# Cross-covariance attention on one core: the K side scaled on GpSimd, logits behind the Gram products, V one unit deeper, closing transposes in other banks

## The chip, the core and the metric

One Trainium2 chip, of which the kernel uses one core. The metric is the device time of one execution in microseconds (us); lower is better. Four executions of the kernel before took 133.0 to 134.84 us, with a median of 133.59 us.

## The reference

Inputs are Q, K and V, each 8 x 12 x 512 x 64 in float32 (batch, heads, sequence, dim). The attention is taken between channels, not between positions:

```python
Q_norm = Q / (np.linalg.norm(Q, axis=-2, keepdims=True) + 1e-10)
K_norm = K / (np.linalg.norm(K, axis=-2, keepdims=True) + 1e-10)
attn = np.einsum('bhnd,bhne->bhde', Q_norm, K_norm)
attn = np.exp(attn - np.max(attn, axis=-1, keepdims=True))
attn = attn / (np.sum(attn, axis=-1, keepdims=True) + 1e-10)
return np.einsum('bhnd,bhde->bhne', V, attn)
```

For each of the 96 heads this is a 64 x 64 matrix of products over 512 positions, a softmax over its rows, and a product of V with it.

## The kernel before

The 96 heads are taken four at a time, so there are 24 units. A unit loads 512 KB each of Q, K and V and stores 512 KB. All 97 transfers are issued by the one queue of SyncE (SP), in the order in which the program writes them.

For unit u the work is this. VectorE (DVE) casts Q and K to bf16 side by side into one tile `qkb` (`cast_q`, line 80, and `cast_k`, line 83). TensorE (PE) multiplies each head's [Q K] with itself, 64 small matmuls into the four-bank PSUM tile `gbuf`, named gram (`grams`, line 94). The diagonal holds the squared norms, the lower left block K^T Q. `norms` takes the diagonal of each head on VectorE (line 106, four instructions) and raises it to the power -1/2 on GpSimd (POOL) (line 111, tile `rq`). `keep_kq` copies the K^T Q block out of PSUM on ScalarE (ACT) (line 99). `scale_k` multiplies it by K's factors (line 116, on VectorE, tile `kqs`), `logits` transposes it on TensorE (line 122, tile `lgdup`), `scale_q` multiplies by Q's factors (line 126), `exps` is the exponential on ScalarE (line 130), and `normalise` sums, inverts and multiplies on VectorE (lines 134, 136, 138, tile `ab`). `doubled` brings a copy of the result to the other 64 partitions, by a matmul with the identity (line 152) and a copy on ScalarE (line 153).

V has its own path. `cast_v` makes it bf16 (line 87, on ScalarE in the loop, on VectorE for the last four units). `vtrans` transposes it with eight TensorE instructions into the PSUM tile `vps` (line 145) and copies it out on ScalarE (line 147, tile `vt`). `outs` multiplies `vt` by `ab` in two halves into two PSUM buffers `po` (line 163) and copies each half to `so` (line 167); `store` writes it.

The order on every engine is the order of the program; no scheduler moves anything. The main loop runs steps s = 0 to 23 (lines 199 to 226). In step s the calls are: loads of Q and K of unit s + 3; loads of V up to unit n1 + 2; stores up to n1 - 4; casts of the new V; `cast_q(s+1)`, `scale_k(s-1)`, `normalise(s-2)`, `grams(s)`, `norms(s)`, `cast_k(s+1)`, `doubled(s-2)`, `keep_kq(s)`, the `outs` that are due, `logits(s-1)`, `scale_q(s-1)`, `exps(s-1)` and the new `vtrans`. Here n1 = `outs_by(s)` counts the units whose `outs` are done by the end of step s; it is 19 after the last step. Lines 227 to 260 then close: `scale_k`, `logits`, `scale_q` and `exps` of unit 23, `normalise` and `doubled` of units 22 and 23, and `outs` of units 19 to 23. In this closing part, copies of `outs` are split between ScalarE and VectorE from unit 20 on.

Buffers matter here: Q and K have five each, V five (`vp`), `vb` four, `vt` three, the output ten. `vps` has one buffer of one bank, `gram` has four banks. `lgdup` is one bank: the logits lie in partitions 0 to 63 of its first half, the doubled matrix in partitions 64 to 127 of its second half.

Of the kernel before, what the change touches and what calls it, by code (L numbers as in the profile page):

```python
# [9 lines left out]
BF16 = mybir.dt.bfloat16  # L10
# [5 lines left out]
HU = 4  # L16
NV = 32
R = 16
SV = 2
MV = 64  # L20
TP = 4
# [3 lines left out]
def kernel(  # L25
# [7 lines left out]
    nc = tc.nc  # L33
    B, H, N, _ = Q.shape
    assert N == NV * R and Q.shape[3] == D
    U = B * H // HU
# [5 lines left out]

    const = ctx.enter_context(tc.tile_pool(name="const", bufs=1))
    qp = ctx.enter_context(tc.tile_pool(name="qp", bufs=5))
    vp = ctx.enter_context(tc.tile_pool(name="vp", bufs=5))
    vbp = ctx.enter_context(tc.tile_pool(name="vbp", bufs=4))
    qkp = ctx.enter_context(tc.tile_pool(name="qkp", bufs=4))
    vtp = ctx.enter_context(tc.tile_pool(name="vtp", bufs=3))
# [3 lines left out]
    ps_v = ctx.enter_context(tc.tile_pool(name="ps_v", bufs=1, space=bass.MemoryType.PSUM))  # L52
# [5 lines left out]
    def outs_by(s):  # L58

        return max(0, (s - 2) * 10 // 11)  # L60
# [10 lines left out]
    def load_v(u):  # L71
        vf[u] = vp.tile([128, SV, TP * 2 * D], F32, name="vf")
        nc.sync.dma_start(out=vf[u], in_=Vf[u])

    def store(u, g=slice(0, SV)):
        nc.sync.dma_start(out=Of[u][:, g], in_=so[u][:, g].rearrange("p s t d -> p s (t d)"))
# [8 lines left out]
    def cast_v(u, copy=nc.scalar.copy):  # L85
        w = vb[u] = vbp.tile([128, SV, TP, 2 * D], BF16, name="vb")
        copy(w.rearrange("p s t d -> p s (t d)"), vf[u])  # L87
# [25 lines left out]
    def scale_k(u):  # L113

        kk = kqs[u] = small.tile([128, HU, D], F32, name="kqs")
        nc.vector.tensor_tensor(  # L116
            out=kk[D:], in0=kq[u][D:], in1=rq[u][D:, :, None].to_broadcast([D, HU, D]), op=ALU.mult,
        )

    def logits(u):  # L120
        for h in range(HU):
            nc.tensor.transpose(lg[:, h, :], kqs[u][D:, h, :], ident[D:, D:])  # L122
# [14 lines left out]
        a = abuf[u % len(abuf)]  # L137
        nc.vector.tensor_tensor(out=a[0:D, :, 0, :], in0=ex[u], in1=ri[:, :, None].to_broadcast([D, HU, D]), op=ALU.mult)  # L138

    def vtrans(u):  # L140

        ps = ps_v.tile([128, SV, TP, 128], BF16, name="vps")
        for g in range(SV):
            for t in range(TP):
                nc.tensor.transpose(ps[:, g, t, :], vb[u][:, g, t, :], identb)  # L145
        w = vt[u] = vtp.tile([128, SV, TP, 128], BF16, name="vt")
        nc.scalar.copy(w, ps)  # L147

    def doubled(u):

        a = abuf[u % len(abuf)]
        nc.tensor.matmul(dup[D:], identb[0:D, 0:D], a[0:D, :, 0, :], tile_position=(0, D))  # L152
        nc.scalar.copy(a[D:, :, 1, :], dup[D:])  # L153

    def outs(u, copies=(nc.scalar.copy, nc.scalar.copy)):
        s = so[u] = sop.tile([128, SV, TP, 2 * D], F32, name="so")
        a = abuf[u % len(abuf)]
        for g in range(SV):
            po = ps_o.tile([128, TP, 2 * D], F32, name="po")
            for t in range(TP):  # L160
                for x in range(2):
                    rows = slice(MV * x, MV * (x + 1))
                    nc.tensor.matmul(  # L163
                        po[rows, t, :], vt[u][:, g, t, rows],
                        a[:, 2 * g + x].rearrange("p a d -> p (a d)"), tile_position=(0, MV * x),
                    )
            copies[g](s[:, g], po)  # L167

    gbuf = ps_g.tile([128, HU, 512], F32, name="gram")
# [20 lines left out]
    def on(f, u):  # L190
        if 0 <= u < U:
            f(u)
# [5 lines left out]
    nv, nst, nt = 2, 0, 0  # L198
    for s in range(U):
        n0, n1 = outs_by(s - 1), outs_by(s)  # L200
        on(load_qk, s + LOAD_AHEAD)
        while nv < min(U, n1 + 3):
            load_v(nv)
            nv += 1
        while nst < n1 - 3:
            store(nst)
            nst += 1
        new = range(nt, n1 + 1) if s >= 1 else ()
        for v in new:
            cast_v(v)  # L210
        on(cast_q, s + 1)
        on(scale_k, s - 1)
        on(normalise, s - 2)
        on(grams, s)
        on(norms, s)
        on(cast_k, s + 1)
        on(doubled, s - 2)
        on(keep_kq, s)
        for v in range(n0, n1):
            outs(v)  # L220
        on(logits, s - 1)
        on(scale_q, s - 1)
        on(exps, s - 1)
        for v in new:
            vtrans(v)
            nt = v + 1
# [8 lines left out]

    last = U - 1
    both = (nc.scalar.copy, nc.vector.tensor_copy)
    scale_k(last)
    logits(last)
    cast_v(n1 + 1, nc.vector.tensor_copy)  # L240
    normalise(last - 1)
# [1 line left out]
    exps(last)  # L243
    outs(n1)
    store(n1)
    vtrans(n1 + 1)
    doubled(last - 1)
    normalise(last)
    doubled(last)
    cast_v(n1 + 2, nc.vector.tensor_copy)  # L250
    for u in range(n1 + 1, U):
        if u + 1 < U:
            vtrans(u + 1)
        if u + 2 < U:
            cast_v(u + 2, nc.vector.tensor_copy)
        outs(u, both)
        if u < last:
            store(u)
# [32 lines left out]
```

## Time and profile before

| | before |
|---|---|
| time, median of four | 133.59 us |
| time of the profiled execution | 133.54 us |
| span in that profile | 131.7 us |
| busy: PE, DVE, ACT, POOL | 68%, 76%, 70%, 32% |
| HBM traffic | 50.3 MB, 382 GB/s over the span |
| mean granted TensorE clock | 0.846 |

The span runs from the first to the last instruction of the program; 1.84 us of the execution's time lie outside it. A row of groups gives the line, the engine, the operation, its tiles and shapes, how often it ran, its busy time and mean duration, and the idle time of the engine ahead of it with what ended that idle time. A row of the timeline gives start, duration, engine, line and operation, and in brackets the idle time before it and its releaser. The stage table gives, for stretches of the span, each engine's busy time (with the number of instructions), then the granted clock, the share of DMA engine time and GB/s.

### The profile page before, as it was taken

The page shows a single profiled execution, that of the slowest core. Times are in us where ns is not written, and L with a number is a line of the kernel's source. Part 1 is how long each engine was busy: PE and PEld are TensorE (multiplying, and loading weights), DVE is VectorE, ACT ScalarE, POOL GpSimd, SP SyncE. Part 2 cuts the span into 40 slices and gives each one's busy share as a digit, 9 for nine tenths or more (in the row PEclk, how much of TensorE's full clock was granted, in tenths as well). Part 3 has the DMA queues.
Part 4 walks back from the last instruction along what each step waited for, and adds up shares of the span by engine and source line. Part 5 has one row for each costly group of instructions (what it writes and reads, how often), then busy time and mean ns, then how long its engine had stood idle before and what let it go on. Part 6 is the DMA issues. An engine that isn't in the chain of part 4 may idle for free.

```text
span 131.7 us, 5371 instructions
## 1 busy us (share of the span) xinstructions
PE 89.8 (68%) x2232; PEld 70.0 (53%) x2232; DVE 100.7 (76%) x368; ACT 92.0 (70%) x161; POOL 41.9 (32%) x41
## 2 busy tenths in 40 slices
PE   0057855799669475959965499666889639577930
PEld 0046733577457354838743387455668528355730
DVE  0757789878899997948999979999979776682540
ACT  3002722478999999849896488999986969866560
POOL 7704432541444323405422363234440430300000
PEclk9999999999999999655899757999856995955595
DMA  4999999999999999999999999999999999998665
GB/s 153 379 417 402 399 409 410 404 397 399 402 397 411 405 417 404 407 400 410 404 415 405 413 409 409 411 407 410 403 415 404 407 405 402 407 403 320 236 262 218
DMA packets 20008, 50.67 MB, mean 385 GB/s; under 512 B 1552, under 2 KB 1552, under 8 KB 19984
## 3 DMA queue, kind: packets, MB, share of 16 engines
q1 hardware_dynamic: 19984, 50.34, 97.9%
q8 instruction: 17, 0.28, 0.8%
q14 instruction: 7, 0.06, 0.1%
HBM read 37.75 MB, written 12.58 MB: 382 GB/s over the span
## 4 chain that ended last, share of the span: by engine, by line
PE 26%; DMA 26%; DVE 24%; POOL 11%; issue 6%; ACT 4%; POOLq 0%; ACTq 0%; DVEq 0%; SPq 0%
DMA vf<-in_V_dram 23%; POOL rq L111 11%; PE gram L94 11%; DVE scr L106 7%; PE vps L145 6%; PE po L163 5%; DVE esum L134 3%; DVE ab L138 3%; DVE kqs L116 3%; DMA qf<-in_Q_dram 3%; PE lgdup L122 2%; ACT vt L147 2%; PE lgdup L152 2%; DVE qkb L80 2%; DVE qkb L83 1%
## 5 line engine op out<-in xcount | busy, mean ns | idle before, releaser
L111 POOL TENSOR_TENSOR rq<-nsq,mhalf 128x4 f32<-128x4 f32 x24 | 36.8, 1532 | 71.5 <-DVE nsq L106 71.5
L94 PE MATMUL gram<-qkb 32*128 32x128 bf16 x1536 | 36.7, 260 | 14.1 <-DVE qkb L83 9.1
L94 PEld LDWEIGHTS <-qkb 32*128 32x128 bf16 x1536 | 30.5, 116 | 18.6 <-DVE qkb L83 9.9
L106 DVE CUSTOM_DVE_ANT_0 scr<-gram,ident 128x128 f32<-128x128 f32 x96 | 22.0, 281 | 5.3 <-PE gram L94 5.1
L147 ACT COPY vt<-vps 128x1024 bf16<-128x1024 bf16 x24 | 24.0, 1002 | 2.4 <-PE vps L145 2.0
L167 ACT COPY so<-po 128x512 f32<-128x512 f32 x44 | 23.8, 588 | 0.8 <-PE po L163 0.4
L87 ACT CAST vb<-vf 128x1024 bf16<-128x1024 f32 x20 | 20.9, 1046 | 4.9 <-DMA vf<-in_V_dram 4.9
L80 DVE CAST qkb<-qf 128x1024 bf16<-128x1024 f32 x24 | 17.9, 745 | 5.6 <-DMA qf<-in_Q_dram 5.5
L163 PEld LDWEIGHTS <-vt 128*64 128x64 bf16 x384 | 14.9, 134 | 12.9 <-ACT vt L147 7.9
L145 PE MATMUL vps<-identb,vb 128*128 128x128 bf16 x192 | 19.4, 262 | 1.3 <-ACT vb L87 0.7
L163 PE MATMUL po<-ab,vt 128*64 128x128 bf16 x384 | 19.3, 259 | 1.1 <-DVE so L167 0.8
L152 PE MATMUL lgdup<-ab,identb 64*64 64x256 bf16 x24 | 8.0, 334 | 16.0 <-DVE ab L138 14.4
L145 PEld LDWEIGHTS <-vb 128*128 128x128 bf16 x192 | 14.6, 118 | 5.5 <-issue 1.6
L153 ACT CAST ab<-lgdup 64x256 bf16<-64x256 f32 x24 | 8.8, 367 | 11.4 <-PE lgdup L152 11.1
L99 ACT COPY kq<-gram 64x256 f32<-64x256 f32 x24 | 8.8, 367 | 11.1 <-DVE nsq L106 10.6
L83 DVE CAST qkb<-kf 128x1024 bf16<-128x1024 f32 x24 | 16.4, 683 | 0.0
L122 PE MATMUL lgdup<-ident,kqs 64*64 64x64 f32 x96 | 11.9, 256 | 5.0 <-ACT ab L153 3.4
L126 DVE TENSOR_TENSOR sl<-lgdup,rq 64x256 f32<-64x256 f32 x24 | 9.9, 414 | 5.7 <-PE lgdup L122 5.1
L130 ACT ACTIVATE ex<-sl 64x256 f32<-64x256 f32 x24 | 10.0, 417 | 4.4 <-DVE sl L126 4.2
L122 PEld LDWEIGHTS lgdup<-ident,kqs 64*64 64x64 f32 x96 | 7.3, 126 | 9.2 <-ACT ab L153 6.3
L116 DVE TENSOR_TENSOR kqs<-kq,rq 64x256 f32<-64x256 f32 x24 | 10.1, 422 | 2.6 <-ACT so L167 0.8
L134 DVE TENSOR_REDUCE esum<-ex 64x4 f32<-64x256 f32 x24 | 9.9, 411 | 1.2 <-ACT ex L130 0.5
(16 smaller groups left out, 36.5 us busy)
## 6 DMA issues: line engine op xcount, KB each, us to landing
qf<-in_Q_dram SPq DMA_DIRECT2D x24, 512.0 KB, 10.4
kf<-in_K_dram SPq DMA_DIRECT2D x24, 512.0 KB, 10.4
vf<-in_V_dram SPq DMA_DIRECT2D x24, 512.0 KB, 10.2
out_dram<-so SPq DMA_DIRECT2D x23, 512.0 KB, 10.1
out_dram<-so SPq DMA_DIRECT2D x2, 256.0 KB, 2.6
```

Source lines behind the costliest of these rows:

```text
L80: nc.vector.tensor_copy(qkb[u][:, :, 0:D], qf[u])
L83: nc.vector.tensor_copy(qkb[u][:, :, D:], kf[u])
L87: copy(w.rearrange("p s t d -> p s (t d)"), vf[u])
L94: nc.tensor.matmul(gbuf[:, h, 0:2 * D], x, x, start=(t == 0), stop=(t == R - 1), tile_position=(NV * h, 0))
L106: nc.vector.tensor_tensor_reduce(out=scr, in0=gbuf[:, h, 0:2 * D], in1=ident, scale=1.0, scalar=1e-20, op0=ALU.mult, op1=ALU.add, accum_ou ...
L111: nc.gpsimd.tensor_tensor(out=r, in0=n2, in1=mhalf, op=ALU.pow)
L116: nc.vector.tensor_tensor(out=kk[D:], in0=kq[u][D:], in1=rq[u][D:, :, None].to_broadcast([D, HU, D]), op=ALU.mult,)
L122: nc.tensor.transpose(lg[:, h, :], kqs[u][D:, h, :], ident[D:, D:])
L145: nc.tensor.transpose(ps[:, g, t, :], vb[u][:, g, t, :], identb)
L147: nc.scalar.copy(w, ps)
L163: nc.tensor.matmul(po[rows, t, :], vt[u][:, g, t, rows], a[:, 2 * g + x].rearrange("p a d -> p (a d)"), tile_position=(0, MV * x),)
L167: copies[g](s[:, g], po)
```

## The change

Four things change.

1. `scale_k` runs on GpSimd, and for unit s in step s, so it stands directly behind `norms(s)`'s power in GpSimd's order. Its call before the closing part goes.
2. In a step, `logits(s-1)`, `scale_q(s-1)` and `exps(s-1)` come directly after `keep_kq(s)`. So TensorE's order becomes grams, logits, outs, doubled, vtrans (before: grams, doubled, outs, logits, vtrans). ScalarE's order becomes keep_kq, exps, outs' copies, doubled's copy, vtrans' copy (before: doubled's copy, keep_kq, outs' copies, exps, vtrans' copy). On VectorE `cast_k(s+1)` comes behind `scale_q(s-1)` in place of ahead of it.
3. V is loaded up to unit n1 + 3, with six buffers in place of five.
4. In the closing part, `vtrans` of units 20 to 23 writes to the four banks of `gbuf` in turn (banks 0, 1, 2, 3) in place of `vps`.

```diff
-    vp = ctx.enter_context(tc.tile_pool(name="vp", bufs=5))
+    vp = ctx.enter_context(tc.tile_pool(name="vp", bufs=6))
...
-        nc.vector.tensor_tensor(
+        nc.gpsimd.tensor_tensor(
             out=kk[D:], in0=kq[u][D:], in1=rq[u][D:, :, None].to_broadcast([D, HU, D]), op=ALU.mult,
         )
...
-    def vtrans(u):
+    def vtrans(u, bank=None):
 
-        ps = ps_v.tile([128, SV, TP, 128], BF16, name="vps")
+        if bank is None:
+            ps = ps_v.tile([128, SV, TP, 128], BF16, name="vps")
+        else:
+            ps = gbuf[:, bank].bitcast(BF16).rearrange("p (s t c) -> p s t c", s=SV, t=TP)
...
-        while nv < min(U, n1 + 3):
+        while nv < min(U, n1 + 4):
             load_v(nv)
...
         on(cast_q, s + 1)
-        on(scale_k, s - 1)
         on(normalise, s - 2)
         on(grams, s)
         on(norms, s)
-        on(cast_k, s + 1)
-        on(doubled, s - 2)
         on(keep_kq, s)
-        for v in range(n0, n1):
-            outs(v)
+        on(scale_k, s)
         on(logits, s - 1)
         on(scale_q, s - 1)
         on(exps, s - 1)
+        on(cast_k, s + 1)
+        for v in range(n0, n1):
+            outs(v)
+        on(doubled, s - 2)
...
-    scale_k(last)
     logits(last)
...
-    vtrans(n1 + 1)
+    vtrans(n1 + 1, 0)
...
         if u + 1 < U:
-            vtrans(u + 1)
+            vtrans(u + 1, (u - n1) % HU)
```

## Prediction, made before the changed kernel ran

> **What bounds the kernel now.** I read the page's busy shares first, then its slices for DMA, because 50.3 MB is much for one core.
>
> ```profile
> PE 89.8 (68%) x2232; PEld 70.0 (53%) x2232; DVE 100.7 (76%) x368; ACT 92.0 (70%) x161; POOL 41.9 (32%) x41
> ...
> DMA  4999999999999999999999999999999999998665
> GB/s 153 379 417 402 399 409 410 404 397 399 402 397 411 405 417 404 407 400 410 404 415 405 413 409 409 411 407 410 403 415 404 407 405 402 407 403 320 236 262 218
> ```
>
> No engine is full, but the DMA engines are, at about 405 GB/s, until the last four slices. SP's timeline has issues 1.27 us apart (512 KB each) and its waits are on earlier transfers; a Q load issued at 94.03 is used at 104.21. So from 3 to 118 us the order and number of transfers set the pace, and work done faster in the middle buys nothing. Only the end can be shortened. The stage table of the end:
>
> ```profile
> 116.00:118.00 2.00, 1.80 (x19) 1.14 (x15) 1.45 (x5) 1.33 (x4) 0.00 (x0) 0.50 1.05 407
> 118.00:120.00 2.00, 0.62 (x5) 0.44 (x6) 1.39 (x3) 1.52 (x4) 0.00 (x0) 0.50 0.98 373
> 120.00:122.00 2.00, 1.84 (x25) 1.50 (x24) 0.24 (x1) 1.34 (x3) 0.00 (x0) 0.50 0.74 282
> 122.00:124.00 2.00, 1.88 (x24) 1.55 (x23) 1.12 (x3) 1.33 (x3) 0.00 (x0) 0.50 0.57 216
> 124.00:126.00 2.00, 1.72 (x24) 1.36 (x23) 0.81 (x2) 1.33 (x2) 0.00 (x0) 0.67 0.63 240
> ```
>
> The queue runs dry from 120 us: stores wait for `outs`. TensorE (first column) is busy 1.84 and 1.88 of 2 us, at half clock (0.50). The last copy ends at 127.92, its store is issued at about 128.1, and the span ends at 131.7: 3.8 us behind the last copy. So the time is decided by when the closing chain ends. Its links in the timeline:
>
> ```profile
> 106.77 1.04 ACT L87 CAST vb<-vf 128x1024 bf16<-128x1024 f32 x1 [1.04 <-DMA vf<-in_V_dram]
> 108.26 0.63 PE L122 MATMUL lgdup<-ident,kqs 64*64 64x64 f32 x4 [0.92 <-ACT ab L153]
> 113.14 1.01 POOL L111 TENSOR_TENSOR rq<-nsq,mhalf 128x4 f32<-128x4 f32 x1 [4.37 <-DVE nsq L106]
> 114.18 0.42 DVE L116 TENSOR_TENSOR kqs<-kq,rq 64x256 f32<-64x256 f32 x1 [0.83 <-ACT so L167]
> 116.67 0.42 ACT L130 ACTIVATE ex<-sl 64x256 f32<-64x256 f32 x1 [1.31 <-DVE sl L126]
> 120.81 1.01 ACT L147 COPY vt<-vps 128x1024 bf16<-128x1024 bf16 x1 [0.66 <-PE vps L145]
> 121.88 1.01 PE L145 MATMUL vps<-identb,vb 128*128 128x128 bf16 x8 [0.16 <-ACT vt L147]
> 124.05 1.01 PE L145 MATMUL vps<-identb,vb 128*128 128x128 bf16 x8 [0.16 <-ACT vt L147]
> 127.23 0.69 DVE L167 COPY so<-po 128x512 f32<-128x512 f32 x1 [0.73 <-PE po L163]
> ```
>
> V of unit 18 comes late (first row), which delays the doubled copy and so the logits (second). VectorE then waits for the power (third, fourth), ScalarE stands 1.31 us for the last exponential (fifth), and the last units alternate transposes and copies (the rest).
>
> [...] the first Q cast took 2.25 us in place of 0.69 while GpSimd's memsets ran, and the power takes 1.01 us alone but 1.46 (median), ending just behind a cast (65.75 behind a cast that ends at 65.72). But that cast began at 65.04, inside the power[...]. [...] logits wait for the copy of the doubled matrix (second row above), which lies in other partitions of that bank. [...] the grant changes at multiples of 3.4 us and was 0.50 from 115.1 to 125.3.
>
> **Scaling on GpSimd.** VectorE loses 24 x 0.42 = 10.1 us, 0.42 a step. The trace shows no such GpSimd instruction. [...] I take 0.7. In the middle: norms end at N, the power is through at N + 1.8 (behind two casts), the scaled tile at N + 2.5. The next logits follow the next grams, at N + 3 or later, so this is hidden under grams; without that cover it would cost TensorE 0.5 us a step. No DMA is issued by GpSimd, and only powers stand behind it.
>
> **The new order.** Logits no longer wait for a doubled copy of the same step (3.4 us of such waits on its matmuls in all). In return `doubled` waits for `scale_q`, with only vtrans behind it, and ScalarE's exponential waits for `scale_q`, about 0.1 us. ScalarE does some 4.0 us of work a step either way (0.37 + 1.07 + 0.42 + 1.0 + 1.05 + 0.37 less overlap). VectorE's step falls from 4.02 to about 3.6, TensorE's at half clock stays 4.9; transfers need 4 x 1.27 = 5.1 in the late part. So the middle stays with DMA: gain zero. If the cover failed, each step over 5.1 us would count in full.
>
> **V one deeper.** One V load moves ahead of Q and K of unit 4 on SP and everything behind it shifts by one transfer: Q of unit 23 lands at 104.2 + 1.3 = 105.5, V of unit 18 at 106.7 - 3.8 = 102.9, stores one place later. V of unit 23 keeps its place in the order, at 118.3. The sixth buffer is free in time (V of unit 17 is cast by 103). So the wait for V goes, and what is late next is Q: VectorE in step 22 runs Q's cast from 105.5, normalise and norms to 108.2 (0.7 + 1.0 + 1.0). Before, norms of that step ended at 107.4, but ScalarE's `keep_kq` began at 108.1 because of V. Now it begins at 108.25: no gain so far.
>
> **The closing part.** ScalarE is then busy without a gap. From start to start (as in the timeline of before), keep_kq, exponential, two outs copies, doubled copy, `vt` and `cast_v` take 0.39 + 0.43 + 0.96 + 0.35 + 0.91 + 1.05 = 4.1, and the same in step 23 up to `vt` 0.39 + 0.4 + 0.96 + 0.35 + 1.0 = 3.1, so `vt` of unit 19 ends at 115.45, as before (115.36). Norms of unit 23 end near 112.2, scaled tile at 114.0, logits behind the doubled copy at 114.5, `scale_q` to 115.5, exponential at 115.6 in place of 116.67. TensorE's outs of unit 19 (1.06) and transposes of 20 (1.03) end at 117.6; ScalarE's copy `vt` of 20 begins at 117.65, against 117.94: gain 0.3. Then units 20 to 23 go at TensorE's pace, 1.03 + 1.06 = 2.1 us a unit at half clock. Before it was 2.17 (121.88 to 124.05), with a wait of 0.16 on the one `vps` bank. With four banks the two waits go: gain up to 0.3, of which I keep 0.1, because the last `outs` also waits for `po` buffers. Where the bank wait goes, TensorE itself is late next. The sum is 0.3 + 0.1, less about 0.1 for the power-and-scaling chain: 0.3 us off 131.7, so a span of 131.4. With 1.84 us around it, 133.2; the profiled time (133.54) is 0.05 below the median, so 133.3.
>
> **Rivals.** [...] If the scaling holds back a Q cast (0.66) and the `ab` product (0.4) each step, VectorE's full-clock step goes from 3.6 to 4.7, against 4.0 now. Before, VectorE catches up with the loads only at unit 21 (cast 0.2 us behind landing), so about 12 full-clock steps lose 0.4 to 0.7 each, 5 to 8, less 1.3 for the later Q and less what catches up: 2 to 5 us, 135.3 to 138. It decides once a full-clock step passes 4.15 us. For it: the 2.25 us cast. Against: the scaling starts behind both casts. Second, faster: the closing runs at full clock[...]; then outs and transposes take 0.64 + 0.62, ScalarE's 1.0 + 0.59 rules, and four units gain 4 x 0.5 = 2.0: about 131.2. [...] Third: the changes hide completely, no bank wait matters, 133.6.
>
> **How the numbers follow.** Forecast 133.3: 0.47, own range 132.6 to 134.0; hides, 133.6: 0.13; [...] a late scaled tile of unit 23 (over 0.8 us of slack) or a worse clock, 134 to 135: 0.07; full clock: 0.13. [...] One per cent, 1.3 us, is about what a measurement of this kernel tells from no change. Faster than 132.25: 0.17. Slower than 134.9: 0.23. Between: 0.6.
>
> **What would show it.** Right: GpSimd's scaling at 0.6 to 0.9 us and VectorE's casts still at 0.68; no ScalarE wait on V late; Q's casts of units 21 to 23 starting at landing; GB/s flat to 118 us; bank waits at line 145 gone and the last copy near 127.6. Wrong: casts or `ab` products over 0.8, Q's casts late by microseconds at unit 23, or the clock at 1.0 in the closing part.

## The result, and the profile after

The changed kernel took 134.18 us (median of 43 executions), the kernel before 133.48 us (64 executions on the same chips): ratio 1.005, 95% interval 1.0033 to 1.0067. So it is slower by 0.5%, some 0.7 us. That is inside the predicted range and inside its 1% case, but with the other sign than the forecast of 133.3 us, and above the forecast's own range (132.6 to 134.0). The prediction did have a case of 134 to 135 us, with a chance of 0.07, for a late scaled tile of unit 23 or a worse clock; neither is what was found, so that this number fits is luck. Executions over 1.5% longer than the fastest of their kernel count as slow: the ratios and intervals in this document leave them out, the medians beside them do not.

The profiled execution of the changed kernel took 133.38 us, 0.8 below its median. Its span (131.6 us, before 131.7) is therefore not set against the one before; landmarks inside the traces are, and medians where a few tenths matter. The page of the changed kernel, busy shares and DMA slices:

```profile
PE 87.1 (66%) x2232; PEld 67.2 (51%) x2232; DVE 89.6 (68%) x344; ACT 95.9 (73%) x161; POOL 67.2 (51%) x65
...
DMA  4999999999999999999999999999999999998675
GB/s 142 381 402 402 399 402 410 406 399 398 404 398 403 407 412 405 410 407 404 408 403 407 417 408 404 408 412 407 410 410 405 410 401 405 403 406 342 263 266 219
```

VectorE lost 11.1 us of work and GpSimd took 25.3 more. ScalarE, from which nothing was taken and to which nothing was given, went from 92.0 to 95.9 us with the same 161 instructions. The DMA slices are as full as they were, to the same place. In the stage table of the end, the answer to that of before, TensorE (first column) is about as busy and at half clock (0.50) from 118 to 124 us; from 124 us on the clock is 0.97, where it was 0.67, so this execution had the better clock at its end:

```profile
116.00:118.00 2.00, 1.44 (x25) 1.16 (x24) 1.28 (x4) 1.91 (x4) 0.00 (x0) 0.82 1.05 407
118.00:120.00 2.00, 0.80 (x4) 0.30 (x4) 1.33 (x3) 1.50 (x3) 0.00 (x0) 0.50 1.03 397
120.00:122.00 2.00, 1.98 (x25) 1.63 (x25) 0.00 (x0) 1.29 (x3) 0.00 (x0) 0.50 0.77 289
122.00:124.00 2.00, 1.86 (x24) 1.57 (x24) 1.29 (x2) 1.33 (x3) 0.00 (x0) 0.50 0.52 200
124.00:126.00 2.00, 1.39 (x28) 1.09 (x24) 1.08 (x2) 1.74 (x4) 0.00 (x0) 0.97 0.63 237
```

The links of the closing chain in the timeline of the changed kernel (lines 145, 147, 152, 153, 163 and 167 of before are now 148, 150, 155, 156, 166 and 170; PEld is TensorE's weight load, and "issue" is idle time for which the profile shows no releaser):

```profile
106.22 0.77 DVE L80 CAST qkb<-qf 128x1024 bf16<-128x1024 f32 x1 [1.34 <-DMA qf<-in_Q_dram]
...
107.57 1.05 ACT L87 CAST vb<-vf 128x1024 bf16<-128x1024 f32 x1
...
108.90 0.37 ACT L99 COPY kq<-gram 64x256 f32<-64x256 f32 x1 [0.28 <-DVE nsq L106]
...
115.61 0.25 PEld L122 LDWEIGHTS lgdup<-ident,kqs 64*64 64x64 f32 x4 [1.93 <-issue]
...
116.61 0.42 ACT L130 ACTIVATE ex<-sl 64x256 f32<-64x256 f32 x1
...
118.20 1.01 ACT L150 COPY vt<-gram 128x1024 bf16<-128x1024 bf16 x1
...
122.14 1.01 PE L148 MATMUL gram<-identb,vb 128*128 128x128 bf16 x8 [0.16 <-ACT vt L150]
...
124.31 0.61 PE L148 MATMUL gram<-identb,vb 128*128 128x128 bf16 x8 [0.16 <-ACT vt L150]
...
127.03 0.69 DVE L170 COPY so<-po 128x512 f32<-128x512 f32 x1 [0.73 <-PE po L166]
```

What was removed and what came: V of unit 18 is no longer waited for (second row, no bracket). In its place VectorE waits 1.34 us for Q of unit 23 (first row), and `keep_kq` of unit 22 waits for the norms behind it (third) and starts at 108.90, where before it was 108.11. The two waits of 0.16 on the copy are still there, now on `gram` in place of `vps`. From the lists of waits, before and then after (engine, line, what was waited for: total us, times, longest):

```profile
DVE qkb L80 <- DMA qf<-in_Q_dram: 5.5, 3, 4.1
...
ACT vb L87 <- DMA vf<-in_V_dram: 4.9, 4, 2.3
```

```profile
DVE qkb L80 <- DMA qf<-in_Q_dram: 9.2, 5, 4.1
...
PEld lgdup L122 <- POOL kqs L116: 7.1, 10, 1.1
...
ACT vb L87 <- DMA vf<-in_V_dram: 2.6, 1, 2.6
```

2.3 us of waits for V went, 3.7 us of waits for Q came. That the trade was a bad one was then a theory; the runs below test it.

### The profile page after: what moved, and what is told of

It reads as the page before. It is cut to its first block, busy times and chain, and to the rows that moved or that the text cites. A ratio compares the mean times of both kernels' runs of the same rounds, so it can differ in the third digit from the quotient of the medians.

```text
span 131.6 us, 5413 instructions
## 1 busy us (share of the span) xinstructions
PE 87.1 (66%) x2232; PEld 67.2 (51%) x2232; DVE 89.6 (68%) x344; ACT 95.9 (73%) x161; POOL 67.2 (51%) x65
## 4 chain that ended last, share of the span: by engine, by line
DMA 37%; PE 22%; ACT 14%; DVE 8%; POOL 8%; issue 7%; SPq 1%; ACTq 0%; POOLq 0%
DMA qf<-in_Q_dram 22%; DMA vf<-in_V_dram 14%; PE gram L94 7%; POOL rq L111 6%; ACT vt L150 5%; PE po L166 5%; DVE scr L106 4%; PE vps L148 4%; ACT so L170 3%; PE gram L148 3%; PE lgdup L122 2%; POOL kqs L116 2%; ACT vb L87 2%; ACT kq L99 2%; PE lgdup L155 1%
## 5 line engine op out<-in xcount | busy, mean ns | idle before, releaser
L111 POOL TENSOR_TENSOR rq<-nsq,mhalf 128x4 f32<-128x4 f32 x24 | 47.4, 1973 | 44.3 <-DVE nsq L106 30.6
L94 PE MATMUL gram<-qkb 32*128 32x128 bf16 x1536 | 35.3, 254 | 17.8 <-DVE qkb L83 9.5
L94 PEld LDWEIGHTS <-qkb 32*128 32x128 bf16 x1536 | 29.3, 113 | 27.1 <-DVE qkb L83 15.3
L80 DVE CAST qkb<-qf 128x1024 bf16<-128x1024 f32 x24 | 18.4, 765 | 9.3 <-DMA qf<-in_Q_dram 9.2
L150 ACT COPY vt<-vps 128x1024 bf16<-128x1024 bf16 x20 | 20.2, 1012 | 0.8 <-PE vps L148 0.3
L148 PEld LDWEIGHTS <-vb 128*128 128x128 bf16 x192 | 13.6, 112 | 10.3 <-ACT vb L87 4.1
L116 POOL TENSOR_TENSOR kqs<-kq,rq 64x256 f32<-64x256 f32 x24 | 14.7, 611 | 2.3 <-POOL rq L111 0.5
L148 PE MATMUL vps<-identb,vb 128*128 128x128 bf16 x160 | 14.8, 246 | 1.3 <-ACT vb L87 1.0
L122 PEld LDWEIGHTS lgdup<-ident,kqs 64*64 64x64 f32 x96 | 7.1, 123 | 10.8 <-POOL kqs L116 7.1
L138 DVE TENSOR_TENSOR ab<-ex,rinv 64x256 bf16<-64x256 f32 x24 | 10.4, 432 | 0.8
```

What stands on the lines that cost most here:

```text
L80: nc.vector.tensor_copy(qkb[u][:, :, 0:D], qf[u])
L94: nc.tensor.matmul(gbuf[:, h, 0:2 * D], x, x, start=(t == 0), stop=(t == R - 1), tile_position=(NV * h, 0))
L111: nc.gpsimd.tensor_tensor(out=r, in0=n2, in1=mhalf, op=ALU.pow)
L116: nc.gpsimd.tensor_tensor(out=kk[D:], in0=kq[u][D:], in1=rq[u][D:, :, None].to_broadcast([D, HU, D]), op=ALU.mult,)
```

## The experiments

Four suspects: the order of steps with its longer ScalarE chain (A), Q and K landing one transfer later behind the deeper V load (B), the GpSimd scaling (C), and stalls in TensorE's supply of instructions (D). Ratios are to the kernel before on the same chip, with 95% intervals.

### Which part of the change costs

V's depth alone, on the kernel before:

```diff
-    vp = ctx.enter_context(tc.tile_pool(name="vp", bufs=5))
+    vp = ctx.enter_context(tc.tile_pool(name="vp", bufs=6))
-        while nv < min(U, n1 + 3):
+        while nv < min(U, n1 + 4):
```

> The kernel before with V one unit deeper (six buffers, up to n1 + 3) and nothing else. Theory B: the later landing of Q costs here as it did in the changed kernel, about 0.5 us: 134.0. Theory D: the pace is that of before, so the compute reaches the loads later than they land and the time is 133.4 to 133.7; what V waits for is saved.

Measured: 134.21 us, 1.0043 [1.0017, 1.0069]. The reverse, the changed kernel with those two lines as they were:

> The changed kernel with V loads as before (five buffers, up to n1 + 2); all else as changed. Theory A: ScalarE's step stays 4.30, the time stays near 134.2, or rises by up to 0.5 because V of unit 18 is late again. Theory B: back to 133.5, since Q of unit 23 lands 1.3 us earlier. Theory C: 134.2.

Measured: 133.69 us, 1.0007 [0.998, 1.0034]. So the deeper V load alone costs about what the whole change costs (0.43% of the 0.5%), and all the rest together costs nothing that can be measured. B stands so far; A and C fall as causes of the loss in the changed kernel as a whole.

The rest is nothing only as a sum. GpSimd scaling alone, with the order of before (`scale_k(s)` directly behind `keep_kq(s)`):

```diff
-        nc.vector.tensor_tensor(
+        nc.gpsimd.tensor_tensor(
...
-        on(scale_k, s - 1)
...
         on(keep_kq, s)
+        on(scale_k, s)
```

> The kernel before with K^T Q scaled on GpSimd behind the power, and nothing else. The changed kernel with the old order was 136.85. If that came from the scaling in the old order (the logits wait late in TensorE's step, so a block of its instructions takes longer than the 6.2 us in which the next arrives): about 136.3 to 136.9. If it came from the deeper V or the banks: 133.4.

Measured: 135.51 us, 1.0124 [1.0077, 1.017]. And the changed kernel with only its order of steps taken back (`cast_k`, `doubled`, then `keep_kq`, `scale_k`, `outs`, and logits, `scale_q` and `exps` behind them):

> The changed kernel with the order of a step as before (cast_k and doubled ahead of keep_kq, outs ahead of logits, exponential behind the outs copies); scaling on GpSimd, V one deeper and the closing banks stay. Theory A (the new order costs ScalarE 0.39 us a step, since its neighbouring copies no longer overlap: 4.30 us from step to step against 3.92 of pure work before): the step falls back to about 4.0 and the time to 133.2 to 133.5. Theory B (Q and K one transfer later): stays at 134.2. Theory C (the GpSimd chain): stays at 134.2 or rises.

Measured: 136.85 us, 1.0241 [1.0195, 1.0287]. The scaling on GpSimd costs 1.2% in the old order, and the new order gives it back. Why it costs that is not shown: in the trace of the scaling alone the logits' weight loads wait for the scaled tile once (1.0 us); the rest of what they wait, 10.8 us in 19 pieces, lies in "issue". This last kernel differs from the one with the scaling alone by the deeper V load and the banks; here they cost 1.2% and not 0.4%. Its trace shows VectorE casting Q of unit 21 2.8 us behind its landing; why the cost is so large was not taken apart.

`keep_kq` of the changed kernel moved to VectorE, to relieve ScalarE (`nc.scalar.copy` to `nc.vector.tensor_copy` at line 99):

> The changed kernel with the copy of K^T Q (keep_kq) on VectorE, behind the norms, in place of ScalarE: 0.39 us and one or two of the lost overlaps leave ScalarE, about 3.7 us a step; VectorE's step rises from 3.6 to 4.0. Theory A: 133.5 or less. Theory B: 134.2, as the landing of Q is unchanged. Theory C: 134.2.

Measured: 135.83 us, 1.0122 [1.0085, 1.016]. Worse; the copy now stands behind the norms on VectorE. Why that costs so much was not taken apart. The run gave a by-product on ScalarE, told at the end.

The kernel before with only the closing transposes changed, alternating between a bank of `gram` and `vps`, which are two tiles and not two banks of one:

```diff
-            vtrans(u + 1)
+            vtrans(u + 1, None if (u - n1) % 2 else 0)
```

> The kernel before, with only its closing transposes changed: units 20 and 22 go to bank 0 of the gram tile, 21 and 23 to vps, so that neighbours lie in different tensors. The waits of 0.16 us ahead of the transposes of units 22 and 23, which the changed kernel kept although it uses four banks, should be gone. If they are worth what the prediction said: 0.1 to 0.3 us faster than before, 133.2 to 133.4. If TensorE and the po buffers cover them: 133.5.

Measured: 133.29 us, 0.9993 [0.9971, 1.0015]. Its transposes no longer wait on the copy (timeline of this kernel, no brackets):

```profile
120.97 1.04 PE L148 MATMUL vps<-identb,vb 128*128 128x128 bf16 x8
...
122.93 1.03 PE L148 MATMUL gram<-identb,vb 128*128 128x128 bf16 x8
...
124.59 0.62 PE L148 MATMUL vps<-identb,vb 128*128 128x128 bf16 x8
```

So four banks of one tile keep the wait, two tiles remove it, and removing it is worth nothing measurable.

Suspect D: grams with each head's 512 positions on 64 partitions (8 steps of 64 rows in place of 16 of 32). That is 32 matmuls a unit fewer, on the kernel before and on the changed one:

```diff
-        for t in range(R):
+        for t in range(R // 2):
             for h in range(HU):
-                x = qkb[u][NV * h:NV * (h + 1), t, :]
+                r = 2 * NV * (h % 2)
+                x = qkb[u][r:r + 2 * NV, R // 2 * (h // 2) + t, :]
```

> The kernel before, with Q and K laid out so that a head takes 64 partitions and 8 rows of each: grams are 32 matmuls over 64 rows in place of 64 over 32, so TensorE has 122 instructions a step in place of 186, with about the same streaming time. Theory D (TensorE's instructions arrive in blocks of 256, one every 6.1 to 6.3 us while the data queue is full, and this sets the pace from 37 to 111 us): the 17 blocks become about 11, the stalls inside grams go, the cast of Q of unit 16 begins at its landing and not 2 us behind it, and the time falls by 0.5 to 1.5 us if the pace also matters at the end, or stays at 133.4 if the loads gate the end anyway. Theory B (only the landing of the last loads counts): 133.4.

> The changed kernel with the same layout and the same 122 instructions of TensorE a step. Theory D: the stalls of 0.5 to 2.6 us inside grams go and with them the loss: 133.4 or less. Theory B: stays at 134.2, since Q still lands one transfer later. Theory A (ScalarE's order): stays near 134.2.

Measured: 136.27 us, 1.0181 [1.0136, 1.0226], and 136.48 us, 1.0205 [1.0159, 1.0251]. The stalls inside the grams went (none in either trace, against 4.8 us before), though in the first kernel the weight loads of `outs` then lost 8.0 us in "issue" (3.5 before). The time rose: Q and K come in rows of 2 KB, not 4, and the queue is slower. The page of the first of the two, DMA rate:

```profile
GB/s 133 350 356 401 387 386 389 387 385 387 382 387 391 399 410 395 398 391 399 404 400 400 404 387 401 401 400 403 398 401 407 404 405 403 407 406 372 251 247 221
```

Compare the slices five to thirteen with those of before: 382 to 391 in place of 397 to 411. V of unit 23 lands at 121.8 us (before 118.3), 3.5 us later, and the median is 2.4 to 3 us worse. Since the loads slowed with it, the pair is no clean test of D. Against D as the cause of the loss stands the run with V's depth alone: it changes no instruction of TensorE and costs about as much as the whole change. That a later landing of the loads passes on to the time fits the pair as well.

### Loads earlier: what rules then

If late loads set the end, stores that give way to loads should shorten it. The kernel before, and the changed one, with stores two units later:

```diff
-        while nst < n1 - 3:
+        while nst < n1 - 5:
```

> The kernel before, with the stores issued two units later (stores up to n1 - 6 in place of n1 - 4), so that every load behind the first stores stands two transfers earlier in the queue. If the arrival of the last loads sets the end: Q of unit 23 lands near 101.7 us in place of 104.2, V of unit 23 near 115.8 in place of 118.3; VectorE's lag behind the landings (2.1 us at unit 16) grows by 2.5 and falls by 0.7 a unit, so about 0.5 is left at unit 23 and the end comes some 2 us earlier: about 131.5 us, ratio 0.985. If the engines' own pace sets the end: at most 0.5 us gained, 133.0 or more. If the stores that are put off pile up behind the last load (10 of 1.27 us from 115.8): they are through near 129, still ahead of the last copy's own store, so no loss; a ratio over 1 would say that they are not.

> The changed kernel, with the stores issued two units later. Loads set the end: Q of unit 23 near 103.7 us in place of 106.2; lag behind landing at unit 16 from 1.1 to 3.6, falling by 0.56 a unit, so hardly any is left at unit 23; the end comes 2.2 us earlier, about 132.0 us, and the cost of the V load one unit deeper is as much as before (0.4 to 0.5 us over the same without it). Engines' pace sets the end: 133.7 or more, and since this kernel's ScalarE takes 4.3 us a step it gains less than the kernel before does with the same edit.

Measured: before with it 132.78 us, 0.9968 [0.9944, 0.9991]; changed with it 133.71 us, 1.0011 [0.9984, 1.0039]. A gain of 0.4 and 0.5 us (the second against the changed kernel as it is), but a fifth to a quarter of the 2 us expected. In the trace of the first (an execution of 133.49 us, 0.7 above its median) the last copy does end 1.6 us earlier (126.3 for 127.9), but the stores that were put off fill the queue (its stage table; the last three numbers are clock, DMA share, GB/s):

```profile
120.00:124.00 4.00, 3.79 (x48) 3.23 (x47) 1.92 (x3) 2.67 (x4) 0.00 (x0) 0.50 0.88 338
124.00:128.00 4.00, 0.82 (x22) 0.58 (x16) 1.38 (x2) 1.41 (x3) 0.00 (x0) 0.93 0.94 358
```

Before, the share in 120 to 128 us was 0.65 and 0.67 in such slices. So the expectation that they would be through near 129 us fell: the last lands at 130.8, 4.4 us behind the last copy.

The changed kernel with stores one unit later (`n1 - 4`), which gives Q of unit 23 its old place back, and the changed kernel with V's depth undone and stores two units later:

> The changed kernel, with the stores issued one unit later: this takes back what the deeper V load did to Q and K (Q of unit 23 at about 104.9 us in place of 106.2) and leaves V one unit early (V of unit 18 near 101.7). If the later Q and K is the whole cost of the deeper V load: the loss of 0.7 us goes, and the wait for V does not come back, so 132.9 to 133.3 us, ratio 0.996 to 0.999. If the loss lies in the new order on ScalarE or in the scaling on GpSimd: it stays at 134.0 to 134.2, ratio 1.004.

> The changed kernel with V's depth as before (five buffers) and the stores issued two units later. Loads set the end: as the kernel before with the same edit or up to 0.3 us off it, 131.5 to 131.8 us. If with loads early the engines' pace rules, the order of the change shows: VectorE has less to do (faster by up to 0.5 us than the kernel before with the same edit) or ScalarE has more (4.3 against 3.9 us a step: slower by 0.3 to 1 us).

Measured: 133.88 us, 1.0034 [1.0009, 1.0058], and 132.87 us, 0.9958 [0.9927, 0.9989]. The first contradicts B as it stood: Q of unit 23 landed at 104.5, as early as in kernels without the deeper load, and the loss stayed outside of what B allowed. The deeper load must cost in a second place.

### Start or end

With the deeper load, one V more stands ahead of Q of unit 4. VectorE waits for that Q at the start: it is cast at 21.3 us in the changed kernel, 19.7 before. (Single traces spread here: it lands at 19.7 to 21.3 us in eleven traces without the early depth and at 21.2 to 22.0 in seven with it, the two kernels with other rows left out.) So the depth was split in time: deeper from step 6 on alone, in the kernel before and in the changed kernel; and deeper in the first six steps alone.

```diff
-        while nv < min(U, n1 + 4):
+        while nv < min(U, n1 + (4 if s >= 6 else 3)):
```

> The kernel before with V one unit deeper from step 6 on alone, so that the first six steps' loads stand as before and the last ones as in the changed kernel. If the deeper load costs at the start: Q of unit 4 lands at about 19.9 us again, the loss of 0.43 per cent goes, ratio 0.998 to 1.001. If it costs at the end (Q of unit 23 landing near 105.5 us): ratio 1.004.

> The changed kernel with V one unit deeper from step 6 on alone. Start: as without the deeper load, ratio 1.000 (0.998 to 1.002), keep_kq of units 4 to 12 earlier by 0.4 to 1.4 us. End: 1.005, as the changed kernel.

> The kernel before with V one unit deeper in the first six steps alone: the last loads stand as before. Start: the whole loss, ratio 1.004, with keep_kq late by over 1 us from unit 3 on and by 0.3 or more still at unit 22. End: no loss, 1.000.

Measured: 134.06 us, 1.0054 [1.0029, 1.0078]; 133.87 us, 1.0061 [1.004, 1.0082]; and 133.49 us, 0.9998 [0.9968, 1.0029]. With stores in their place the whole loss is at the end and none that can be measured at the start. In the trace of the third kernel `keep_kq` is 1.8 us later than before at unit 3 and 0.6 us at unit 22, and the median does not move; the kernel with two tiles, whose loads stand as before, was 1.6 us late at unit 3 in its trace, so part of this is spread. The end in the timeline of the first kernel, ScalarE and VectorE:

```profile
106.28 0.69 DVE L80 CAST qkb<-qf 128x1024 bf16<-128x1024 f32 x1 [1.06 <-DMA qf<-in_Q_dram]
...
106.88 1.05 ACT L87 CAST vb<-vf 128x1024 bf16<-128x1024 f32 x1
108.88 0.37 ACT L153 CAST ab<-lgdup 64x256 bf16<-64x256 f32 x1 [0.95 <-PE lgdup L152]
109.40 0.37 ACT L99 COPY kq<-gram 64x256 f32<-64x256 f32 x1 [0.16 <-DVE nsq L106]
```

V of unit 18 is there (it landed at 103.7), and ScalarE gets nothing from it: it stands 0.95 us for the doubled matrix and 0.16 for the norms, both of which stand behind the Q cast on VectorE.

The changed kernel with late depth and stores two units later:

> The changed kernel with V one unit deeper from step 6 on alone and the stores two units later. Start: as the kernel with V's depth undone and the stores two units later, ratio 0.995 to 0.997, some 133.0 us. End: as the changed kernel with the stores two units later, 1.001, some 133.7 us.

Measured: 132.77 us, 0.9954 [0.9931, 0.9977], against 1.0011 with the depth in all steps. Here the start is the whole loss. So it looks as if there were two rules, and which one holds depends on the loads: the step at the end begins with the later of its loads and of what the engines still carry from the start. Two last runs asked whether this one sentence covers the run that contradicted B, and whether one unit or two is the better distance for stores without the deeper load:

> The changed kernel with V one unit deeper from step 6 on alone and the stores one unit later, so Q and K of the last units land as in the kernel before and the start is as in the kernel before. If the end follows the later of load arrival and the engines' backlog from the start: 1.000 or less (0.997 to 1.000), keep_kq of unit 22 near 108.2 us. If something else in the deeper load costs: 1.003 to 1.004, as with the deeper load in all steps.

> The changed kernel with V's depth as before and the stores one unit later. If the last loads' arrival alone rules: half of what two units gave, 0.998. If the stores that are put off fill the queue to the end (as with two units, where they land 1.25 to 1.3 us apart from 118 us to the end): one unit less of them gives as much or more, 0.994 to 0.996.

Measured: 133.03 us, 0.9964 [0.9942, 0.9986], and 132.54 us, 0.9939 [0.9914, 0.9965]. The first agrees: the same kernel with the early steps as before loses nothing (1.0034 became 0.9964, and the intervals lie apart), so with loads early it is the depth of the first six steps that costs. That it costs as a backlog of the engines is read from single traces. With stores one unit later `keep_kq` of unit 12 starts at 65.1 us with the early depth and 64.1 without, of unit 22 at 108.75 and 107.97, although without it Q of unit 23 landed later (105.35 for 104.48). With stores two units later it is 64.9 and 63.7, then 108.43 and 107.95. The second is the fastest of all, 0.6% under the kernel before and about 1.1% under the changed one (0.9939/1.005), though its interval overlaps those of the other four kernels with later stores and no early depth; one unit or two is not told apart. All in one table (GpSimd scaling, new order and banks go together as "new"):

| V depth | stores | order before | new |
|---|---|---|---|
| as before | as before | 1 | 1.0007 |
| as before | 1 later | not run | 0.9939 |
| as before | 2 later | 0.9968 | 0.9958 |
| deeper | as before | 1.0043 | 1.0050 |
| deeper | 1 later | not run | 1.0034 |
| deeper | 2 later | not run | 1.0011 |
| deeper from step 6 | as before | 1.0054 | 1.0061 |
| deeper from step 6 | 1 later | not run | 0.9964 |
| deeper from step 6 | 2 later | not run | 0.9954 |
| deeper to step 5 | as before | 0.9998 | not run |

Why no more was to be had: the stage table of the fastest kernel, and its last copy.

```profile
122.00:124.00 2.00, 1.78 (x34) 1.37 (x30) 0.71 (x2) 1.67 (x3) 0.00 (x0) 0.79 0.90 346
124.00:126.00 2.00, 0.68 (x16) 0.62 (x16) 1.23 (x2) 1.53 (x3) 0.00 (x0) 1.00 0.85 322
126.00:128.00 2.00, 0.00 (x0) 0.00 (x0) 0.13 (x1) 0.00 (x0) 0.00 (x0) 1.00 1.04 388
```

```profile
125.44 0.69 DVE L170 COPY so<-po 128x512 f32<-128x512 f32 x1 [0.77 <-PE po L166]
```

The last copy ends at 126.13, 1.8 us ahead of before, but the span is 131.0: 4.9 us behind the copy, where it was 3.8. The last stores now land some 1.25 to 1.35 us apart, one behind the other, to 130.0 us (the two halves of unit 23 0.64 apart). The queue is the bound up to the end.

## Why the prediction was wrong, by its own steps

**The step that failed is "V one deeper", with its verdict "no gain so far".** It saw both sides of the trade (V's wait goes, Q is late next) and sized them as 108.1 against 108.25. `keep_kq` of unit 22 in the traces with stores in place, without four kernels: `keep_kq` moved, the order undone (engines 2.8 us behind), and the two with other rows.

| | Q of 23 lands | V of 18 lands | `keep_kq` of 22 |
|---|---|---|---|
| without late depth: before | 104.19 | 106.7 | 108.11 |
| changed, V undone | 104.88 | 107.4 | 108.53 |
| two tiles | 105.46 | 108.0 | 109.38 |
| scaling alone | 104.52 | 107.0 | 108.38 |
| V deeper to step 5 | 104.75 | 107.3 | 108.67 |
| mean | 104.76 | 107.3 | 108.61 |
| with late depth: changed | 106.20 | 103.0 | 108.90 |
| V alone | 105.75 | 103.2 | 108.90 |
| V deeper from step 6 | 106.25 | 103.7 | 109.40 |
| changed, V from step 6 | 106.76 | 104.2 | 109.38 |
| mean | 106.24 | 103.5 | 109.15 |

The means of `keep_kq` moved by 0.53 us, and the medians lost about as much (0.43% of 133.5 is 0.57), but Q's landing alone spreads by 1.3 us from trace to trace. The distance from Q's landing to `keep_kq` spreads less. With the order before it was 3.92 us in three traces, because of V (3.86 with the scaling alone), and 3.15 in the two with late depth, because of VectorE: 0.77 gained on the wait, one transfer of 1.27 paid, a loss of 0.5. With the new order it was 3.65, then 2.70 and 2.62: 0.99 gained, a loss of 0.3. The prediction had 0.15. Its distance after, 108.25 - 105.5 = 2.75, was right; its distance before, 3.9, was that of the kernel before, and the rest of the change had already taken 0.25 of it. And it then gave even the 0.15 no term in the sum: it set the chain from `keep_kq` on as "`vt` of unit 19 ends at 115.45, as before", and a gain behind it. In the new order 0.3 of the 0.57 is accounted for in this way; the rest would be that Q landed 1.6 and not 1.3 us later in these three traces, and whether that is more than spread stays open.

**"ScalarE does some 4.0 us of work a step either way"** was mis-sized: 4.3 after. Start to start from the doubled copy (line 156) to the next, less a wait of 0.75 us, is 92.65 - 87.62 - 0.75 = 4.28 us in the trace of the changed kernel; from exponential to exponential it was 90.62 - 86.61 = 4.01 before. From `keep_kq` of unit 22 to the end of `vt` of unit 19 it takes 7.6 us in the changed kernel and in the one with V undone, 7.25 before, 7.0 with V alone; predicted 7.2. With the later `keep_kq` that ate the predicted 0.3 at `vt` of unit 20 (118.20, predicted 117.65, before 117.94). What the new order gains is ahead of it: with late depth, from Q's cast to `keep_kq` 2.6 and 2.7 us in the two kernels with the scaling off VectorE, 3.1 in the two with it. That the two cancel fits the run with V undone (1.0007), which holds both.

**The four banks** gained nothing of the 0.1. That accesses are held apart by bank was the author's estimate; `lgdup`, on whose waits it leaned, is one tile in one bank, so the trace of before did not tell bank from tile. Four banks of one tile still wait (0.16 us twice), and with two tiles the waits went, so in this program they go by tile. The median did not move even then.

**The scaling on GpSimd** came out near the prediction: 0.611 us (median; 0.610 to 0.621) for 0.7, which was the author's estimate and shown by no trace of before. The power ahead of it did not. At unit 23 it is through at N + 1.8 (norms end at 112.0, power at 113.8), but the median over the units is N + 2.4, and the scaled tile is ready at N + 3.1 where the prediction had N + 2.5: the power itself takes 2.25 us (median) in the changed kernel, 1.46 before. So the cover was thinner than told: ten times the logits' weight load waited for the scaled tile, up to 1.1 us, 7.1 us in all (list of waits). In the middle that cost nothing that can be measured, as the run with V undone shows. The prediction did not see that the scaling needs the new order (+1.2% without it, where the tile was waited for once).

**The rivals.** The slower one (135.3 to 138 us, with a chance of 0.2) had the scaling hold back a cast and a product of VectorE in each step; that was the author's estimate, and of the kernel before only the first Q cast, 2.25 us beside GpSimd's memsets, spoke for it. VectorE was not held back: Q casts 678 ns for 675 (medians), nothing lost in the changed kernel with V undone. What took longer was GpSimd's power (mean 1.53 us before, 1.97 in the changed kernel, 1.96 with V undone), and that goes with the new order more than with the scaling (1.62 with the order undone); what it waits for is not shown. The clock was 0.50 in 118 to 124 us; at 0.97 from 124 us on, full clock came for the last unit alone (its transposes took 0.61 us for 1.01); what sets the clock is not shown. "The changes hide" is nearest, and true of three of the four parts.

**"From 3 to 118 us the order and number of transfers set the pace, and work done faster in the middle buys nothing"** held with stores in their place: the depth of the first six steps alone cost nothing that can be measured, though `keep_kq` was late by over a microsecond in its trace. It holds no longer once the loads come 1.3 to 2.5 us earlier (1.0011 against 0.9954). **"Only the end can be shortened"** was right and incomplete: a last copy 1.8 us earlier brought the median down by 0.6%, because the stores then fill the queue. The forecast of the exponential of unit 23 at 115.6 failed by a microsecond (116.61). Its logits started at 115.6 in place of 114.5. The doubled copy had ended at 115.50, late with ScalarE's chain, and their weight load lay 1.93 us in "issue"; both ended within about 0.1 us, so which of them held is not told apart.

## What to carry to other kernels

On a queue that is full, as this one is to 118 us, a deeper prefetch of one tensor is a later arrival of every other: price it as one transfer's time (here 1.27 us) against the wait that it removes, in the stage where both are waited for, and give the difference a line in the sum. Ask also which rule holds there (the last loads' arrival, the engines' backlog, the stores at the end), because an edit that costs nothing under one costs in full under another (here the depth of the first six steps: 0.9998 with stores in their place, 1.0011 against 0.9954 with stores two units later). To bring loads forward, move what nobody waits for: in the new order, stores one unit later (0.9939) gained here what the deeper V load was meant to, and more.

## What the runs showed of the hardware

**ScalarE's neighbours overlap only sometimes.** A step of the same instructions took 4.01 us in the order before and 4.28 in the new one. ScalarE's timeline, kernel before, changed, and changed with `keep_kq` on VectorE:

```profile
89.28 0.37 ACT L99 COPY kq<-gram 64x256 f32<-64x256 f32 x1
89.67 1.07 ACT L167 COPY so<-po 128x512 f32<-128x512 f32 x2
90.62 0.42 ACT L130 ACTIVATE ex<-sl 64x256 f32<-64x256 f32 x1
90.94 0.99 ACT L147 COPY vt<-vps 128x1024 bf16<-128x1024 bf16 x1
```

```profile
91.11 0.42 ACT L130 ACTIVATE ex<-sl 64x256 f32<-64x256 f32 x1 [0.75 <-DVE sl L126]
91.55 1.07 ACT L170 COPY so<-po 128x512 f32<-128x512 f32 x2
92.65 0.37 ACT L156 CAST ab<-lgdup 64x256 bf16<-64x256 f32 x1
```

```profile
87.57 0.42 ACT L130 ACTIVATE ex<-sl 64x256 f32<-64x256 f32 x1 [0.23 <-DVE sl L126]
87.89 1.04 ACT L170 COPY so<-po 128x512 f32<-128x512 f32 x2
88.96 0.37 ACT L156 CAST ab<-lgdup 64x256 bf16<-64x256 f32 x1
```

After the exponential (0.42 us) the next copy starts 0.32 us later in the first and third, 0.44 in the second, with the same two instructions in second and third. What differs is the instruction ahead of them: `keep_kq`, which lies in partitions 64 to 127, in the second only. The medians of all neighbouring pairs without a wait, in the traces before and after, say this. Where the copies that read PSUM lie in partitions from 0 on (`outs`' copies and `vt`, with the exponential or V's cast between or behind them), an instruction starts about 0.1 us before the end of the one ahead. Where `keep_kq` or the doubled copy, both in partitions 64 to 127, is the one ahead, the one behind, or the last to have read PSUM, it starts about 0.02 us after that end. Where `keep_kq` follows the doubled copy, four of thirteen pairs before overlap by 0.09 or 0.10 us, and the others start 0.00 to 0.13 us after the end. In the order before two of the seven neighbours in a step are of the second kind, or three with this pair, in the new order five: at 0.12 us each, 0.25 to 0.37 us, for the 0.27 measured. That the partitions are the cause fits these pairs and the run with `keep_kq` moved; no run was made for it alone.

**TensorE's breaks inside the grams follow the instruction packets.** Timeline of the changed kernel:

```profile
55.09 1.01 PE L94 MATMUL gram<-qkb 32*128 32x128 bf16 x58
58.67 0.29 PE L94 MATMUL gram<-qkb 32*128 32x128 bf16 x6 [2.58 <-issue]
```

Such breaks inside the grams come 256 instructions (matmuls and weight loads) or a multiple of it apart (512, 256 and 512 between the four of the kernel before). The trace's instruction queue moves 17 packets of 16 KB, against 4464 recorded matmuls and weight loads, 263 to a packet. A packet takes 0.9 to 1.1 us, and the breaks inside the grams end 1.3 to 1.6 us after one has moved. From 43 to 112 us one comes every 5.9 to 6.5 us, but at 186 instructions a step of about 4.5 us TensorE uses up 256 in as long, so this does not tell whether the full data queue holds them up. Whether the breaks cost time here stays open: the kernel without breaks in the grams had slower loads as well.

**Rows of 2 KB in place of 4 KB** took the one queue from 397 to 411 GB/s down to 382 to 391 in slices five to thirteen (some 13 to 44 us).
